# Storing block 0's x, B, C weights, block 0's z through ScalarE, two query loads, and a dealt gate norm in a hybrid attention and state-space layer

## The chip, the cores and the metric

The kernel runs on one core of a Trainium2 chip. The metric is the device time of one launch in microseconds (us). A core has five engines that matter here: TensorE (PE in the profile, matmuls from SBUF into PSUM), VectorE (DVE), ScalarE (ACT), GpSimd (POOL) and SyncE (SP), whose queue issues the DMA transfers. Each engine runs its own instructions in program order and waits on semaphores for the others.

## The reference, cut to what matters

One layer: 2048 frames of a new stream and 32 frames of a running one, 1024 channels. Half of the mixer is stick-breaking attention (8 heads of 64), half is a Mamba-2 scan (SSD, 8 heads of 64, state 64), both from one input projection; then a gated convolutional MLP.

```python
def mixer(h, k_past, v_past, ssm_h0, conv_prev, p):
    proj = h @ p['w_in']                       # q, k, v, z, xbc, dt_raw in this order
    ...
    attn = stick_breaking(q, q_pos, k_all, v_all, k_pos).reshape(b, l, D_ATT)
    xbc_c, conv_new = causal_dwconv(xbc, conv_prev, p['ssm_conv_w'], p['ssm_conv_b'])
    xbc_c = jax.nn.silu(xbc_c)                 # x (512), B (128), C (128)
    ...
    y, h_fin = ssd_scan(xh, dt, a, bm, cm, ssm_h0)
    y = y + p['d_skip'][:, None] * xh
    y = rmsnorm(y * jax.nn.silu(z), p['g_ssm_out'])
    out = jnp.concatenate([rmsnorm(attn, p['g_attn_out']), y], axis=-1) @ p['w_out']

def layer(x, ...):
    x = x + rmsnorm(mixer(rmsnorm(x, p['g_mix_pre']), ...), p['g_mix_post'])
    return x + rmsnorm(conv_ffn(rmsnorm(x, p['g_ffn_pre']), ...), p['g_ffn_post'])
```

The rows of a normalisation share one factor r = rsqrt(mean of squares + eps), so a projection can be taken of x * gain and multiplied by r afterwards. Block 0 does this.

## The kernel before, in words

**Numbers as pairs.** Every matmul with a weight is three matmuls of float32r parts: high times high, high times low, low times high (`dense`, rows of L173). A weight becomes such a pair by `divide` (L148): ScalarE casts the raw block to its high part (L153), GpSimd subtracts to get the low part (L154), and if a key is given, SyncE stores the pair in DRAM as `wS_<key>` (L157). Later `weight` finds the key and `recall`s the pair by one DMA (L145). In the input phase a weight block is 128 columns by all 8 blocks of 128 channels: 512 KB raw, 1 MB as a pair. There are two raw buffers and three pair buffers.

**Blocks.** `phase_in` goes over four blocks of the sequence (512, 512, 512, and 544 with the running stream's 32 frames). In each it projects x, B, C (six column blocks in the order 4, 5, 0, 1, 2, 3; 4 and 5 are B and C, the tile `bc`; 0 to 3 are x, the tile `xc`). Each column block is 24 matmuls into a PSUM bank `o` (two of these), a ScalarE copy out of it (L397), in block 0 a multiplication by r (L401), four convolution steps on VectorE (L404, L408) and a silu (ScalarE's sigmoid L388, VectorE's product L389), one column block late. Then come v and dt (L432), the scan in chunks of 128 frames (its first product is L520, of C with B; acB is its decay matrix), k and q (stored to DRAM), and the gate. `prep(s + 1)` loads the next block's x, and normalises it (L322); `split` makes its pairs (ScalarE L331, VectorE L332).

**Gate.** `gate` (L631) projects z in four column blocks and multiplies xc by silu(z): sigmoid L653, products L654 and L656. For block 0, L647 first multiplies by r, out of PSUM. For blocks 1 and 2 ScalarE copies z to SBUF (`zc`). `gate_norm` (L661) takes squares, one factor, and per column block a product (L677), a cast (L681) and a subtraction (L683), stored as `yS`. Block 3's gate is not run there: it is handed to the attention phase as a filler.

**Attention.** `heads(s, steps)` walks slots, one per 128 query rows and key block: products z (L890), sigmoids on ScalarE, a running product on VectorE (L741), transposes (L909), two copies (L913 on ScalarE, L914 on VectorE) and the products with v (L931). `steps` filler steps are dealt evenly over the slots: heads(0) has 32 slots and deals the 32 steps of block 3's gate, six matmuls each. Every third slot also advances `sample`, the running stream's attention, whose first work is to zero `qp`, load the query into it head by head (L764) and load keys (L786, tile `sk`). After heads(0) the last gate norm runs to its end, in PSUM bank `u`; then `stream(0)`, the output projection and MLP of block 0, is the filler of heads(1), and so on. The last stream runs alone.

**Order.** The code above is program order; a list scheduler with its own cost estimates then sets each engine's order. `behind(a, b)` adds an order between two instructions without a semaphore of its own.

Of the kernel before, what the change touches and what calls it, by code (L numbers as in the profile page):

```python
# [8 lines left out]
F32 = mybir.dt.float32  # L9
# [3 lines left out]
ALU = mybir.AluOpType  # L13
# [18 lines left out]
P = 128  # L32
D = 1024
KC = D // P
SEQ = 2048
DEC = 32
TOK = SEQ + DEC
NH = 8
DH = 64
# [6 lines left out]
NSB = len(SBS)  # L46
# [23 lines left out]
class Kernel:  # L70
# [77 lines left out]
    def divide(self, pool, raw, m, key=None, tag=None):  # L148

        nc = self.nc  # L150
        w = self.held(pool, tag)
        hi, lo = w[:, 0, :m, :], w[:, 1, :m, :]
        nc.scalar.copy(hi, raw[:, :m, :])  # L153
        nc.gpsimd.tensor_tensor(lo, raw[:, :m, :], hi.bitcast(F32), op=ALU.subtract)  # L154
        if key is not None:
            d = self.dp.tile([P, 2, m, P], F32, name="wS_" + "_".join(map(str, key)))
            nc.sync.dma_start(d[:], w[:, :, :m, :].bitcast(F32))  # L157
            self.kept[key] = d[:]
            if m > UNIT:
                for i in range(0, m, UNIT):  # L160
                    self.kept[(*key[:-1], "part", i)] = d[:, :, i : i + UNIT, :]
        return [(w[:, 0, i, :], w[:, 1, i, :]) for i in range(m)]
# [102 lines left out]
def phase_in(kn, ctx):  # L265
    nc, tc, a, o = kn.nc, kn.tc, kn.a, kn.o
    pool = lambda name, bufs, **kw: ctx.enter_context(tc.tile_pool(name=name, bufs=bufs, reuse_waits="tile", **kw))
# [6 lines left out]
    wp = kn.wp  # L274
# [88 lines left out]
        else:  # L363
            nc.scalar.copy(dst, ps)

    wfirst = kn.weight(wp, a["wbx"][4])
    for s, (t0, nt) in enumerate(SBS):
        last = s == NSB - 1
        if s == 0:
            xs, r0 = first()  # L370
# [17 lines left out]
            kn.behind(nc.scalar.activation(t[:, :W], y, AF.Sigmoid), copy)  # L388
            nc.vector.tensor_tensor(y, y, t[:, :W], op=ALU.mult)  # L389

        for c in (4, 5, 0, 1, 2, 3):
            w = wfirst if s == 0 and c == 4 else kn.weight(wp, a["wbx"][c], key=("bx", c) if s or c in (1, 2, 3) else None)
            for c0, c1 in tiles_of(nt):
                ps = psd.tile([P, 512], F32, name="o")
                kn.dense(ps, w, xs, c0, c1)
                e = min(c1, 512)
                copy = nc.scalar.copy(raw[:, c, 3 + c0 : 3 + e], ps[:, : e - c0])  # L397
                if c1 > 512:
                    copy = nc.scalar.copy(raw[:, c, 518:550], ps[:, e - c0 : c1 - c0])
            if s == 0:  # L400
                nc.vector.tensor_tensor(raw[:, c, 3 : 3 + nt], raw[:, c, 3 : 3 + nt], r0[:, :nt], op=ALU.mult)  # L401
            y = xc[:, c, :W] if c < 4 else bc[:, c - 4, :W]
            wc = C_SW + c * 4
            nc.vector.tensor_scalar(  # L404
                y, raw[:, c, 0:W], kn.col(wc), kn.col(C_SB + c), op0=ALU.mult, op1=ALU.add
            )
            for i in range(1, 4):
                nc.vector.scalar_tensor_tensor(  # L408
                    y, raw[:, c, i : i + W], kn.col(wc + i), y, op0=ALU.mult, op1=ALU.add
                )  # L410
            if owed is not None:
                silu(owed, copy)
            owed = y
        if last:
            nc.sync.dma_start(o["sconv"][0], raw[:, :, 512:515])
            nc.sync.dma_start(o["sconv"][1], raw[:, :, 547:550])
        else:
            nc.vector.tensor_copy(hist[:], raw[:, :, 512:515])
# [58 lines left out]
        ps = psm.tile([P, 512], F32, name="st")  # L477
# [140 lines left out]
        if last:  # L618
            return lambda tm, pool: (
                gate(kn, s, xs, xc, None, tm),  # L620
                gate_norm(kn, s, xc, tm, lambda sq, *r: kn.rstd_narrow(pool, *kn.bank, [sq], *r)),
            )
        bufs = {"khi": 2, "klo": 2, "t": 2, "sq": 1, "zc": 2}
        tm = lambda nm: (so if nm in ("khi", "klo") else tmp).tile([P, 550 if nm == "t" else 544], F32, name=nm, bufs=bufs[nm])
# [6 lines left out]
def gate(kn, s, xs, xc, r0, tm):  # L631
# [3 lines left out]
    for c in range(4):  # L635
        w = kn.weight(kn.wp, kn.a["wz"][c], key=("z", c) if s < NSB - 1 else ("z", c, "part"))
        for c0, c1 in tiles:
# [4 lines left out]
                if len(tiles) == 1 or k % 2:  # L642
                    yield
            t = tm("t")
            if r0 is not None:
                z = tm("t")
                nc.vector.tensor_tensor(z[:, :n], ps[:, :n], r0[:, c0:c1], op=ALU.mult)  # L647
                ps = z
            elif s < NSB - 1:
                z = tm("zc")  # L650
                nc.scalar.copy(z[:, :n], ps[:, :n])
                ps = z
            nc.scalar.activation(t[:, :n], ps[:, :n], AF.Sigmoid)  # L653
            nc.vector.tensor_tensor(t[:, :n], ps[:, :n], t[:, :n], op=ALU.mult)  # L654
# [3 lines left out]
                nc.gpsimd.tensor_tensor(xc[:, c, 512:544], xc[:, c, 515:547], t[:, e - c0 : n], op=ALU.mult)  # L658


def gate_norm(kn, s, xc, tm, rstd):  # L661

    nc, nt = kn.nc, SBS[s][1]
    sq = tm("sq")
    for c in range(4):
# [5 lines left out]
            nc.gpsimd.tensor_tensor(sq[:, :nt], sq[:, :nt], t[:, :nt], op=ALU.add)  # L671
        yield
    r = rstd(sq, nt, 512)
    for c in range(4):
        yield
        n = xc[:, c, :nt] if s == NSB - 1 else tm("zc")[:, :nt]
# [11 lines left out]
class Attention:  # L688
# [60 lines left out]
    def sample(self, ctx, pu):  # L749
# [9 lines left out]
            )  # L759
        qp = kp.tile([P, 4, DH], F32, name="qp", bufs=1)  # L760
        nc.vector.memset(qp[:], 0.0)
        for h in range(NH):
            r = slice(64 * (h % 2), 64 * (h % 2) + 64)
            nc.sync.dma_start(qp[r, h // 2, 32 * (h % 2) : 32 * (h % 2) + 32], kn.qF[r, h // 2, :])  # L764
        own = []
        for g in range(2):
            own.append([kp.tile([P, w], F32, name=f"{nm}{g}", bufs=1) for nm, w in (("sgam", 513), ("sbeta", 512), ("sprow", 513))])
# [731 lines left out]
def build(nc, tc, a, o):  # L1499
    kn = Kernel(nc, tc, a, o)  # L1500
    with ExitStack() as ctx:
# [24 lines left out]
        att = Attention(kn, heads)  # L1526
        kn.bank = pu, "u"
        late = ssd.enter_context(tc.tile_pool(name="ssd_tmp", bufs=2, reuse_waits="tile", side="right"))
        att.filler, normed = rest(lambda nm: late.tile([P, 544], F32, name=nm, bufs=1 if nm == "sq" else 2), late)
        with ExitStack() as c2:  # L1530
            sample = att.sample(c2, pu)

            out = att.heads(0, KC * 4, lambda i: i % 3 == 2 and next(sample, None))
            for _ in sample:
                pass
        for _ in normed:
            pass
        ssd.close()
        tail = Tail(kn, att, ctx, pu)
        for s in range(NSB):  # L1540
# [106 lines left out]
```

## Time and profile before

| what | us |
|---|---|
| median of three runs | 2916.16 |
| lowest and highest of them | 2910.60, 2920.89 |
| the profiled execution, its own time | 2923.02 |
| its span, first to last instruction | 2921.2 |
| VectorE, ScalarE, GpSimd busy | 1636.6, 1221.8, 1151.0 |

The profile comes from one execution. Times in its rows count from the span's start. Block 0 of the input phase lasts to about 181, blocks 1, 2 and 3 to about 320, 480 and 606; heads(0) follows to about 735. "PEclk" is the share of full clock that TensorE was granted in a stretch. "`<-`" in brackets names what an engine waited for before the row. PE's matmuls overlap, so rows of them may overlap too. SPq rows are DMA issues, not transfers.

### The profile page before, as it was taken

How to read it: one execution, taken by the hardware profiler on the slowest of the kernel's cores; microseconds unless marked ns; L12 is line 12 of the kernel's file. 1: busy time of each engine (PE TensorE's matmuls, PEld its weight loads, DVE VectorE, ACT ScalarE, POOL GpSimd, SP SyncE). 2: the span in 40 equal slices, each digit the busy share in tenths (PEclk: the TensorE clock that was granted, in tenths of full speed). 3: DMA queues.
4: the chain of work that ended last, by engine and by line, in shares of the span. 5: the costliest groups of instructions: out<-in, count | busy, mean ns of one | idle time of the engine just before them, and what ended most of it. 6: DMA issues, size and time to landing. Idle time of an engine off the chain costs nothing.

```text
span 2921.2 us, 46172 instructions
## 1 busy us (share of the span) xinstructions
PE 2806.3 (96%) x16771; PEld 2427.1 (83%) x16771; DVE 1636.6 (56%) x2628; ACT 1221.8 (42%) x2575; POOL 1151.0 (39%) x1076
## 2 busy tenths in 40 slices
PE   7989999979899999999899999989999999999998
PEld 6768889967878888897788888978888889899997
DVE  7584747448664545457454556776666653623333
ACT  4343434247665545455333334654444443321211
POOL 4634242225766656555322223453322323411113
PEclk9999999999989999999999999999999999999999
DMA  7878776868677777785655556666555555755556
GB/s 270 266 267 245 238 241 205 235 191 289 241 249 256 267 275 257 254 284 186 211 176 175 183 181 227 205 197 200 171 164 172 169 167 189 238 180 180 170 177 205
DMA packets 336708, 632.08 MB, mean 216 GB/s; under 512 B 73594, under 2 KB 193026, under 8 KB 328162
## 3 DMA queue, kind: packets, MB, share of 16 engines
q1 hardware_dynamic: 336482, 629.13, 66.4%
q8 instruction: 134, 2.20, 0.3%
q14 instruction: 92, 0.75, 0.1%
HBM read 472.44 MB, written 156.57 MB: 215 GB/s over the span
## 4 chain that ended last, share of the span: by engine, by line
PE 78%; DMA 9%; DVE 7%; SPq 2%; ACT 2%; issue 2%; POOL 1%; DVEq 0%; ACTq 0%; POOLq 0%
PE o L173 39%; PE u L173 12%; PE t L173 11%; PE z L890 4%; PE pa L931 4%; PE pt L909 3%; PE o L432 3%; DMA acB<-acD 2%; DMA w<-wS_out 1%; DVE prow L741 1%; DMA xr<-hS 1%; DMA wraw<-wbx 1%; DVE xlo L1079 1%; DMA o_kT<-kf 1%; PE u L215 1%
## 5 line engine op out<-in xcount | busy, mean ns | idle before, releaser
L173 PE MATMUL o<-xhi,w 128*128 128x512 f32 (+2 forms) x3968 | 1047.2, 345 | 28.8 <-ACT xhi L346 7.7
L173 PEld LDWEIGHTS o<-xhi,w 128*128 128x128 f32 x3968 | 698.1, 191 | 121.6 <-issue 10.8
L173 PE MATMUL o<-xlo,w 128*128 128x512 f32 (+2 forms) x1984 | 683.0, 344 | 3.0 <-DVE xlo L1079 1.6
L746 POOL TENSOR_TENSOR beta<-beta,prow 128x512 f32<-128x512 f32 (+3 forms) x256 | 255.4, 998 | 448.2 <-DVE prow L741 365.8
L173 PEld LDWEIGHTS o<-xlo,w 128*128 128x128 f32 x1984 | 379.4, 191 | 46.7 <-DVE xlo L1079 2.4
L173 PE MATMUL o<-ah,w 128*128 128x512 f32 x992 | 345.0, 404 | 8.2 <-DVE f L1375 6.8
L173 PE MATMUL u<-xhi,w 128*128 128x512 f32 x1056 | 348.7, 397 | 0.0
L154 POOL TENSOR_TENSOR w<-wraw,w 128x512 fp32r<-128x512 f32 (+3 forms) x189 | 253.8, 1346 | 163.9 <-ACT w L153 143.0
L1327 POOL TENSOR_TENSOR y<-y,gb 128x512 f32<-128x512 f32 (+1 forms) x88 | 115.9, 1317 | 508.4 <-ACT gb L1326 508.2
L914 DVE TENSOR_TENSOR wt<-pt,wt 128x512 fp32r<-128x512 f32 (+2 forms) x320 | 191.2, 601 | 170.3 <-ACT wt L913 168.2
L741 DVE TENSOR_TENSOR_SCAN prow<-gam,prow,z 128x513 f32<-128x513 f32 x192 | 245.1, 1277 | 60.9 <-ACT beta L739 57.1
L913 ACT CAST wt<-pt 128x512 fp32r<-128x512 f32 (+2 forms) x320 | 167.1, 526 | 220.6 <-PE pt L909 219.3
L173 PEld LDWEIGHTS u<-xhi,w 128*128 128x128 f32 x1056 | 198.8, 188 | 46.7
L173 PEld LDWEIGHTS o<-ah,w 128*128 128x128 f32 x992 | 187.7, 189 | 50.6 <-DVE f L1375 8.3
L738 ACT ACTIVATE gam<-z 128x512 f32<-128x512 f32 (+2 forms) x320 | 172.7, 540 | 100.2 <-PE z L890 57.0
L173 PE MATMUL u<-xlo,w 128*128 128x512 f32 x528 | 209.3, 396 | 0.0
L173 PE MATMUL o<-al,w 128*128 128x512 f32 x496 | 197.2, 398 | 0.0
L173 PE MATMUL t<-xhi,w 128*128 128x272 f32 x960 | 189.2, 293 | 2.8 <-DMA w<-wS_up 1.8
L153 ACT CAST w<-wraw 128x512 fp32r<-128x512 f32 (+3 forms) x189 | 117.5, 622 | 169.2 <-PE o L173 103.5
L931 PE MATMUL pa<-wt,v 128*64 128x256 f32 (+3 forms) x1152 | 174.1, 282 | 11.6 <-DVE wt L914 10.6
L909 PE MATMUL pt<-ident,beta 128*128 128x128 f32 x1088 | 180.9, 278 | 2.3 <-DVE wt L914 1.9
L1319 DVE SCALAR_TENSOR_TENSOR y<-gb,cv,y 128x512 f32<-128x512 f32 (+1 forms) x176 | 142.2, 808 | 68.4 <-ACT y L1317 65.9
(285 smaller groups left out, 4899.5 us busy)
## 6 DMA issues: line engine op xcount, KB each, us to landing
w<-wS_up SPq DMA_DIRECT2D x264, 512.0 KB, 3.5
w<-wS_dn SPq DMA_DIRECT2D x144, 384.0 KB, 3.5
wS_up<-w SPq DMA_DIRECT2D x88, 512.0 KB, 3.5
w<-wS_out SPq DMA_DIRECT2D x78, 512.0 KB, 6.1
wraw<-wup SPq DMA_DIRECT2D x88, 256.0 KB, 4.1
k<-kS SPq DMA_DIRECT2D x80, 256.0 KB, 3.8
v<-vS SPq DMA_DIRECT2D x80, 256.0 KB, 3.7
wS_dn<-w SPq DMA_DIRECT2D x48, 384.0 KB, 3.1
```

What stands on the lines that cost most here:

```text
L153: nc.scalar.copy(hi, raw[:, :m, :])
L154: nc.gpsimd.tensor_tensor(lo, raw[:, :m, :], hi.bitcast(F32), op=ALU.subtract)
L173: mm = nc.tensor.matmul(ps[:, : c1 - c0], l, r, start=first and i == 0 and k == 0, stop=last and i == 2 and k == len(w) - 1, **({"skip_gro ...
L738: nc.scalar.activation(g[:, c0:512], z, AF.Sigmoid, scale=-0.125)
L741: nc.vector.tensor_tensor_scan(back(pr), back(g), z[:, 0:1].to_broadcast([P, n + 1]), self.kn.ones[:, 0:1] if prev is None else prev, op0= ...
L746: eng.tensor_tensor(b[:, :n], b[:, :n], pr[:, c0 + 1 : 513], op=ALU.mult)
L890: mm = nc.tensor.matmul(z[:, :n], q[:, P * b : P * b + P], k[:, :n], start=e == 0, stop=e == 1 and kc < s)
L909: mm = nc.tensor.transpose(t[:, P * j : P * j + P], w[:, P * j : P * j + P], kn.ident[:])
L913: nc.scalar.copy(hi, t)
L914: nc.vector.tensor_tensor(lo, t, hi.bitcast(F32), op=ALU.subtract)
L931: nc.tensor.matmul(av[:m, 2 * P * p + c0 : 2 * P * p + 2 * P], v[:, j, :m], wt[:, rest, j, c0:], start=kc == s and p + j + rest == 0, stop ...
L1319: nc.vector.scalar_tensor_tensor(y[:, :W], gb[:, i : i + W], kn.col(wc + i), y[:, :W], op0=ALU.mult, op1=ALU.add)
```

## The change

Four edits:

1. In block 0 all six x, B, C weights get a key, so the pairs of 4, 5 and 0 are stored too, and block 1 recalls all six. Also in block 0, the next column block's weight (`ahead`) is loaded, cast and subtracted in program order before the current matmuls, and the exit copy is put behind its cast.
2. Block 0's z is copied out of PSUM by ScalarE, as in blocks 1 and 2, and multiplied by r in SBUF.
3. `qp` is loaded by two DMAs (all even heads, all odd heads) instead of eight.
4. The last gate norm becomes part of heads(0)'s filler: 4 steps of squares, 4 empty steps (`rests`) behind its factor, 4 steps of products, so 44 in all, and its factor uses the PSUM bank `o`.

```diff
--- before.py
+++ after.py
@@ -150,7 +150,7 @@
         nc = self.nc
         w = self.held(pool, tag)
         hi, lo = w[:, 0, :m, :], w[:, 1, :m, :]
-        nc.scalar.copy(hi, raw[:, :m, :])
+        self.cast = nc.scalar.copy(hi, raw[:, :m, :])
         nc.gpsimd.tensor_tensor(lo, raw[:, :m, :], hi.bitcast(F32), op=ALU.subtract)
         if key is not None:
             d = self.dp.tile([P, 2, m, P], F32, name="wS_" + "_".join(map(str, key)))
@@ -363,7 +363,7 @@
         else:
             nc.scalar.copy(dst, ps)
 
-    wfirst = kn.weight(wp, a["wbx"][4])
+    wfirst = kn.weight(wp, a["wbx"][4], key=("bx", 4))
     for s, (t0, nt) in enumerate(SBS):
         last = s == NSB - 1
         if s == 0:
@@ -388,13 +388,21 @@
             kn.behind(nc.scalar.activation(t[:, :W], y, AF.Sigmoid), copy)
             nc.vector.tensor_tensor(y, y, t[:, :W], op=ALU.mult)
 
-        for c in (4, 5, 0, 1, 2, 3):
-            w = wfirst if s == 0 and c == 4 else kn.weight(wp, a["wbx"][c], key=("bx", c) if s or c in (1, 2, 3) else None)
+        order = (4, 5, 0, 1, 2, 3)
+        w = wfirst if s == 0 else None
+        for c, then in zip(order, (*order[1:], None)):
+            if w is None:
+                w = kn.weight(wp, a["wbx"][c], key=("bx", c))
+            ahead = None
+            if s == 0 and then is not None:
+                ahead = kn.weight(wp, a["wbx"][then], key=("bx", then))
             for c0, c1 in tiles_of(nt):
                 ps = psd.tile([P, 512], F32, name="o")
                 kn.dense(ps, w, xs, c0, c1)
                 e = min(c1, 512)
                 copy = nc.scalar.copy(raw[:, c, 3 + c0 : 3 + e], ps[:, : e - c0])
+                if ahead is not None:
+                    kn.behind(copy, kn.cast)
                 if c1 > 512:
                     copy = nc.scalar.copy(raw[:, c, 518:550], ps[:, e - c0 : c1 - c0])
             if s == 0:
@@ -411,6 +419,7 @@
             if owed is not None:
                 silu(owed, copy)
             owed = y
+            w = ahead
         if last:
             nc.sync.dma_start(o["sconv"][0], raw[:, :, 512:515])
             nc.sync.dma_start(o["sconv"][1], raw[:, :, 547:550])
@@ -618,7 +627,7 @@
         if last:
             return lambda tm, pool: (
                 gate(kn, s, xs, xc, None, tm),
-                gate_norm(kn, s, xc, tm, lambda sq, *r: kn.rstd_narrow(pool, *kn.bank, [sq], *r)),
+                gate_norm(kn, s, xc, tm, lambda sq, *r: kn.rstd_narrow(pool, kn.po, "o", [sq], *r), 4),
             )
         bufs = {"khi": 2, "klo": 2, "t": 2, "sq": 1, "zc": 2}
         tm = lambda nm: (so if nm in ("khi", "klo") else tmp).tile([P, 550 if nm == "t" else 544], F32, name=nm, bufs=bufs[nm])
@@ -642,13 +651,11 @@
                 if len(tiles) == 1 or k % 2:
                     yield
             t = tm("t")
-            if r0 is not None:
-                z = tm("t")
-                nc.vector.tensor_tensor(z[:, :n], ps[:, :n], r0[:, c0:c1], op=ALU.mult)
-                ps = z
-            elif s < NSB - 1:
+            if s < NSB - 1:
                 z = tm("zc")
                 nc.scalar.copy(z[:, :n], ps[:, :n])
+                if r0 is not None:
+                    nc.vector.tensor_tensor(z[:, :n], z[:, :n], r0[:, c0:c1], op=ALU.mult)
                 ps = z
             nc.scalar.activation(t[:, :n], ps[:, :n], AF.Sigmoid)
             nc.vector.tensor_tensor(t[:, :n], ps[:, :n], t[:, :n], op=ALU.mult)
@@ -658,7 +665,7 @@
                 nc.gpsimd.tensor_tensor(xc[:, c, 512:544], xc[:, c, 515:547], t[:, e - c0 : n], op=ALU.mult)
 
 
-def gate_norm(kn, s, xc, tm, rstd):
+def gate_norm(kn, s, xc, tm, rstd, rests=0):
 
     nc, nt = kn.nc, SBS[s][1]
     sq = tm("sq")
@@ -671,6 +678,8 @@
             nc.gpsimd.tensor_tensor(sq[:, :nt], sq[:, :nt], t[:, :nt], op=ALU.add)
         yield
     r = rstd(sq, nt, 512)
+    for _ in range(rests):
+        yield
     for c in range(4):
         yield
         n = xc[:, c, :nt] if s == NSB - 1 else tm("zc")[:, :nt]
@@ -759,9 +768,9 @@
             )
         qp = kp.tile([P, 4, DH], F32, name="qp", bufs=1)
         nc.vector.memset(qp[:], 0.0)
-        for h in range(NH):
-            r = slice(64 * (h % 2), 64 * (h % 2) + 64)
-            nc.sync.dma_start(qp[r, h // 2, 32 * (h % 2) : 32 * (h % 2) + 32], kn.qF[r, h // 2, :])
+        for e in range(2):
+            r = slice(DH * e, DH * e + DH)
+            nc.sync.dma_start(qp[r, :, DEC * e : DEC * e + DEC], kn.qF[r, :, :])
         own = []
         for g in range(2):
             own.append([kp.tile([P, w], F32, name=f"{nm}{g}", bufs=1) for nm, w in (("sgam", 513), ("sbeta", 512), ("sprow", 513))])
@@ -1526,15 +1535,13 @@
         att = Attention(kn, heads)
         kn.bank = pu, "u"
         late = ssd.enter_context(tc.tile_pool(name="ssd_tmp", bufs=2, reuse_waits="tile", side="right"))
-        att.filler, normed = rest(lambda nm: late.tile([P, 544], F32, name=nm, bufs=1 if nm == "sq" else 2), late)
+        att.filler = chained(*rest(lambda nm: late.tile([P, 544], F32, name=nm, bufs=1 if nm == "sq" else 2), late))
         with ExitStack() as c2:
             sample = att.sample(c2, pu)
 
-            out = att.heads(0, KC * 4, lambda i: i % 3 == 2 and next(sample, None))
+            out = att.heads(0, KC * 4 + 12, lambda i: i % 3 == 2 and next(sample, None))
             for _ in sample:
                 pass
-        for _ in normed:
-            pass
         ssd.close()
         tail = Tail(kn, att, ctx, pu)
         for s in range(NSB):
```

SyncE and ScalarE at the front of block 0. SyncE's rows before, from behind the second raw weight and the first wv part (`wraw<-wbx` is a raw x, B, C weight, `wS_bx` a stored pair, `x<-xT` a quarter of block 1's input, `wk` a weight of k):

```order
L130 DMA wraw<-wbx 128x1024 x2
L294 DMA wvraw<-wv 128x1040
L311 DMA x<-xT 128x2x512 x2
L130 DMA wraw<-wbx 128x1024
L311 DMA x<-xT 128x2x512 x2
L157 DMA wS_bx_0_353<-w 128x2048
L130 DMA wraw<-wbx 128x1024
L294 DMA wvraw<-wv 128x1040
L157 DMA wS_bx_0_394<-w 128x2048
L130 DMA wraw<-wk 128x1024
L157 DMA wS_bx_0_435<-w 128x2048
```

and after, from the same place (each `wS_bx` is the pair of one weight, in the order 4, 5, 0, 1, 2):

```order
L157 DMA wS_bx_0_160<-w 128x2048
L130 DMA wraw<-wbx 128x1024
L157 DMA wS_bx_0_246<-w 128x2048
L130 DMA wraw<-wbx 128x1024
L294 DMA wvraw<-wv 128x1040
L311 DMA x<-xT 128x2x512 x4
L157 DMA wS_bx_0_284<-w 128x2048
L130 DMA wraw<-wbx 128x1024
L157 DMA wS_bx_0_325<-w 128x2048
L130 DMA wraw<-wbx 128x1024
L294 DMA wvraw<-wv 128x1040
L157 DMA wS_bx_0_366<-w 128x2048
```

Three more stores stand in the queue, each ahead of the next raw weight, and block 1's input is now loaded ahead of the raw weight of column block 2 in one piece.

ScalarE there, before, from the cast of weight 2 (L153; L260 copies r, L295 casts a wv part):

```order
L153 CAST w<-wraw 128x1024
L397 COPY raw<-o 128x512
L260 COPY r_229<-st 128x512
L153 CAST w<-wraw 128x1024
L397 COPY raw<-o 128x512
L295 CAST wvhi<-wvraw 128x1040
L153 CAST w<-wraw 128x1024
L397 COPY raw<-o 128x512
L388 ACT_TABLE_LOAD
L388 ACTIVATE t<-bc 128x512 x2
```

and after (from the exit copy, now L403, on):

```order
L403 COPY raw<-o 128x512
L260 COPY r_231<-st 128x512
L153 CAST w<-wraw 128x1024
L403 COPY raw<-o 128x512
L388 ACT_TABLE_LOAD
L388 ACTIVATE t<-bc 128x512
L153 CAST w<-wraw 128x1024
L388 ACTIVATE t<-bc 128x512
L295 CAST wvhi<-wvraw 128x1040
L388 ACTIVATE t<-xc 128x512
L403 COPY raw<-o 128x512
```

The exit copies follow casts of a later weight, and the cast of weight 3 (the second L153 here; before it stood ahead of the table load) now follows the table load and the first sigmoid of bc.

VectorE at the end of block 0's gate. Before, from the last chunk of the scan (L564, L567) on; L322 normalises block 1's input, L332 splits it:

```order
L532 TENSOR_TENSOR acB<-acB,cbm 128x512 x2
L564 SCALAR_TENSOR_TENSOR xc<-xc,cv,eA 128x128 x4
L322 SCALAR_TENSOR_TENSOR x<-x,cv,rstd 128x512 x8
L647 TENSOR_TENSOR t<-o,r_229 128x512
L567 TENSOR_TENSOR xc<-y,xc 128x4x128
L654 TENSOR_TENSOR t<-t 128x512
L656 TENSOR_TENSOR xc<-xc,t 128x512
L647 TENSOR_TENSOR t<-o,r_229 128x512
L654 TENSOR_TENSOR t<-t 128x512
L656 TENSOR_TENSOR xc<-xc,t 128x512
L647 TENSOR_TENSOR t<-o,r_229 128x512
L332 TENSOR_TENSOR xlo_1611<-x,xhi_1603 128x512
```

and after (L658 multiplies z by r, L661 and L663 are the two products):

```order
L573 SCALAR_TENSOR_TENSOR xc<-xc,cv,eA 128x128 x4
L658 TENSOR_TENSOR zc<-zc,r_231 128x512
L661 TENSOR_TENSOR t<-zc,t 128x512
L576 TENSOR_TENSOR xc<-y,xc 128x4x128
L663 TENSOR_TENSOR xc<-xc,t 128x512
L658 TENSOR_TENSOR zc<-zc,r_231 128x512
L661 TENSOR_TENSOR t<-zc,t 128x512
L322 SCALAR_TENSOR_TENSOR x<-x,cv,rstd 128x512 x8
L663 TENSOR_TENSOR xc<-xc,t 128x512
L658 TENSOR_TENSOR zc<-zc,r_231 128x512
L332 TENSOR_TENSOR xlo_1621<-x,xhi_1613 128x512
```

The eight L322 moved from ahead of the first z to behind the second, and no row reads z out of PSUM.

VectorE where the last gate norm's products stand. Before, in heads(1) (L741 is the running product of a slot, L914 half of its copy):

```order
L914 TENSOR_TENSOR wt<-pt,wt 128x4x128
L741 SCALAR_TENSOR_TENSOR prow<-gam_5846,ones,z 128x129
L746 TENSOR_TENSOR beta<-beta,prow 128x128
L914 TENSOR_TENSOR wt<-pt,wt 128x4x128
L741 SCALAR_TENSOR_TENSOR prow<-gam_5844,ones,z 128x257
L914 TENSOR_TENSOR wt<-pt,wt 128x4x128
L741 SCALAR_TENSOR_TENSOR prow<-gam_5845,ones,z 128x385
L677 SCALAR_TENSOR_TENSOR xc<-xc,cv,rstd 128x544 x4
L914 TENSOR_TENSOR wt<-pt,wt 128x4x128
L228 TENSOR_SCALAR rn_v<-u 128x2
L741 SCALAR_TENSOR_TENSOR prow<-gam_5846,ones,z 128x513
```

and after, in heads(0) (L750 is the running product, `sprow` that of the running stream):

```order
L923 TENSOR_TENSOR wt<-pt,wt 128x4x128
L750 SCALAR_TENSOR_TENSOR prow<-gam_5841,ones,z 128x513
L923 TENSOR_TENSOR wt<-pt,wt 128x128
L955 TENSOR_TENSOR att<-pa,att 64x512
L923 TENSOR_TENSOR wt<-pt,wt 128x2x128
L686 SCALAR_TENSOR_TENSOR xc<-xc,cv,rstd 128x544 x4
L750 SCALAR_TENSOR_TENSOR sprow_5992<-sgam_5990,scarry_5995,z 128x513
L750 SCALAR_TENSOR_TENSOR prow<-gam_5839,ones,z 128x129
L750 SCALAR_TENSOR_TENSOR prow<-gam_5840,ones,z 128x257
L923 TENSOR_TENSOR wt<-pt,wt 128x3x128
L750 SCALAR_TENSOR_TENSOR prow<-gam_5841,ones,z 128x385
```

The four products moved ahead by about 11 running products; they still stand in one piece.

## The prediction

> **What bounds the kernel now.** I read the page first: span, busy shares and the chain that ended last.
>
> ```profile
> span 2921.2 us, 46172 instructions
> ...
> PE 2806.3 (96%) x16771; PEld 2427.1 (83%) x16771; DVE 1636.6 (56%) x2628; ACT 1221.8 (42%) x2575; POOL 1151.0 (39%) x1076
> ...
> PE 78%; DMA 9%; DVE 7%; SPq 2%; ACT 2%; issue 2%; POOL 1%; DVEq 0%; ACTq 0%; POOLq 0%
> ```
>
> TensorE (PE) is busy for 96% of the span and holds 78% of the chain. The change removes no matmul, so it can only close holes in TensorE's work: 2921.2 - 2806.3 = 115 us in all. Next I read TensorE's waits over the first 900 us, where every edit lies. The columns are total, times, longest.
>
> ```profile
> PE z L789 <- DMA sk<-kF: 7.0, 1, 7.0
> PE pa L931 <- DVE wt L914: 6.3, 2, 4.8
> PE o L173 <- DVE t L647: 6.0, 1, 6.0
> ...
> PE y L520 <- DVE bc L389: 2.5, 1, 2.5
> PE o L173 <- DMA w<-wS_bx: 2.3, 1, 2.3
> ```
>
> Four of these five belong to the edited places: L789 to the query loads, L931 to the gate norm, L647 to block 0's z, wS_bx to the weights. The sum of the four longest waits is 7.0 + 4.8 + 6.0 + 2.3 = 20 us. Third view: windows over these holes and the stretches behind them (length, TensorE busy, granted clock, DMA share, GB/s).
>
> ```profile
> 55.00:58.00 3.00, 3.00 (x16) 0.51 0.68 259
> 160.80:163.60 2.80, 2.78 (x7) 0.50 0.68 234
> 190.80:193.60 2.80, 0.48 (x3) 1.00 1.01 427
> 193.60:197.00 3.40, 3.40 (x10) 0.63 0.81 335
> 616.30:623.20 6.90, 0.02 (x1) 0.85 0.10 15
> 623.20:628.00 4.80, 4.80 (x21) 0.50 0.87 256
> 735.10:739.80 4.70, 0.00 (x0) 0.72 0.53 205
> 739.80:745.00 5.20, 5.03 (x21) 0.59 0.40 134
> ```
>
> A hole costs twice here: behind each, the matmuls run for 3 to 5 us at about half clock. That is (1 - 0.50) x 2.8 = 1.4 us behind the z hole, 0.37 x 3.4 = 1.3 behind the recall, 0.5 x 4.8 = 2.4 behind the query loads. Even the 2.5 and 2.3 us waits (L520, wS_bx) are followed by 0.51 and 0.63.
>
> **1. Block 0's x, B, C weights.** Three more stores of 1 MB in block 0; in block 1 three weights come back by one load of 1 MB each, in place of a raw load, a cast (L153), a subtraction (L154) and a store. In block 0 each weight's load, cast and subtraction are issued ahead of the matmuls of the column block before it, and that block's exit copy stands behind the cast.
>
> ```profile
> 15.60 6.14 POOL L154 TENSOR_TENSOR w<-wraw,w 128x1024 fp32r<-128x1024 f32 x2 [6.51 <-ACT w L153]
> ...
> 31.21 1.05 ACT L153 CAST w<-wraw 128x1024 fp32r<-128x1024 f32 x1 [2.67 <-DMA wraw<-wbx]
> ...
> 39.54 1.05 ACT L153 CAST w<-wraw 128x1024 fp32r<-128x1024 f32 x1 [6.31 <-DMA wraw<-wbx]
> ...
> 40.67 2.42 POOL L154 TENSOR_TENSOR w<-wraw,w 128x1024 fp32r<-128x1024 f32 x1 [5.94 <-ACT w L153]
> ...
> 46.06 1.28 ACT L388 ACT_TABLE_LOAD   x1
> 48.96 0.63 ACT L388 ACTIVATE t<-bc 128x512 f32<-128x512 f32 x1 [1.62 <-DVE bc L408]
> ...
> 41.10 2.53 DVE L401 TENSOR_TENSOR raw<-raw,r 128x512 f32<-128x512 f32 x1 [0.60 <-ACT raw L397]
> ...
> 32.20:48.40 16.20, 16.20 (x72) 1.00 0.91 346
> ...
> 100.00:150.00 50.00, 48.26 (x291) 36.61 (x289) 36.08 (x81) 15.93 (x23) 25.04 (x16) 1.00 0.98 321
> ```
>
> The first window says that column blocks 1, 2 and 3 (72 matmuls, 5.4 us each) ran from 32.2 to 48.4 without a hole; their weights were ready in time. A loaded queue moves 427 GB/s (window 190.8), so 512 KB take 1.2 us and 1 MB 2.5. In the new SyncE order the store of column block 5 waits for its subtraction (ends at 15.60 + 6.14 = 21.74), and behind it stand a raw weight, one wv part, four x loads, the store of block 0 and then the raw weight 2: 2.5 + 1.2 + 1.2 + 4.9 + 2.5 + 1.2 = 13.5, so weight 2 lands near 36, against 31.2. Cast 1.05 and subtraction 2.4 put its third matmul at 39.6, where TensorE arrives at 37.6: **2 us** of waiting. Weight 3's cast now stands on ScalarE behind the table load and the first sigmoid of bc. I put that sigmoid at 44.5: before it ran at 48.96 after VectorE had lost some 2 us to each of the operations that took 2.5 (L401 above; 0.68 is usual for this size, as in L647 below), and fewer of them now come ahead. Then cast to 46.2, subtraction to 48.7: matmuls that ended at 48.4 end near 54. Since the scan's first products (L520) move in among them, their own 2.5 us wait lies inside this one. Net, the step behind L520 begins some 3 us later, and 1 us more goes in half clock: **+4**, from 0 (loads early, sigmoid early) to +10 (bc no earlier than before, two more holes at half clock). From there on TensorE hardly waits (48.26 of 50 us busy up to 150), so nothing takes this back.
>
> In block 1 the wait for wS_bx goes, with its half clock: -2.3 - 1.3 = **-3.6**. Its three recalls are issued ahead of block 2's x loads, and no cast or subtraction replaces them. They hide behind the end of block 0's gate; without this cover the old 2.3 returns.
>
> **2. Block 0's z.** VectorE (DVE) read z out of PSUM (L647), and stood in eight L322 while TensorE wanted the bank.
>
> ```profile
> 152.62 7.46 DVE L322 SCALAR_TENSOR_TENSOR x<-x,cv,rstd 128x512 f32<-128x512 f32 x8
> 160.00 0.68 DVE L647 TENSOR_TENSOR t<-o,r 128x512 f32<-128x512 f32 x1
> ...
> 160.71 0.63 ACT L653 ACTIVATE t<-t 128x512 f32<-128x512 f32 x1 [4.84 <-DVE t L647]
> ...
> 183.45 0.57 ACT L397 COPY raw<-o 128x512 f32<-128x512 f32 x1
> ...
> 178.94 2.78 DVE L656 TENSOR_TENSOR xc<-xc,t 128x512 f32<-128x512 f32 x1
> ...
> 178.19 2.98 POOL L154 TENSOR_TENSOR w<-wraw,w 128x1024 fp32r<-128x1024 f32 x1 [3.44 <-ACT w L153]
> ```
>
> Now a ScalarE copy frees the bank. ScalarE gains four copies (0.57 us, as L397), where it sat idle for 4.84 us before the first sigmoid; VectorE keeps its count. The hole of 6.0 and its 1.4 at half clock go. What is late next is the normalised input of block 1: the L322 now come after the second z, some 5 us later, and block 1's split (L332, eight of 0.68) behind them. TensorE has the third and fourth z (10.3 us) and finds the first split operands about 1.5 us late: -7.4 + 1.4 = **-6**, from -2 (the split sets the start) to -7.4.
>
> The last two rows carry a rule: an L656 that began inside a GpSimd (POOL) subtraction took 2.78 and ended as that ended. The Trainium skill (SBUF — State Buffer, "SBUF: two separate sides") says that a VectorE operation with two SBUF inputs and a GpSimd operation that reads SBUF exclude each other for a whole instruction. That speaks against this edit, since z leaves PSUM before it is multiplied: by the page each of four multiplies may lose up to 2 us, on VectorE alone. By the rows the next operation, L656, has two such inputs already. I leave the sum as it is.
>
> **3. Two query loads instead of eight.**
>
> ```profile
> 616.05 4.92 SPq L764 DMA_DIRECT2D qp<-qF  x8
> 621.01 1.06 SPq L786 DMA_DIRECT2D sk<-kF  x2
> ...
> 623.18 0.39 PE L789 MATMUL z<-sk,qp 128*64 128x32 f32 x2 [6.97 <-DMA sk<-kF]
> ```
>
> SyncE spends 4.92 / 8 = 0.62 us on each issue, and the loads that TensorE waits for are queued behind all eight. Six fewer: 6 x 0.62 = **-3.7**. qp's zeroing lets the first go no earlier than 616.05. The hole shrinks to 3.2 us; a 2.3 us wait already cost half clock above, so I keep the 2.4 behind it. Bounds: 0 (the larger loads land that much later) and -6.1.
>
> In the Trainium skill (TensorE: Matmul & The Clock Gate, "Why this matters for your kernels") gaps under about 3 us keep the clock. By that page a slightly smaller hole would spare the 2.4 too. The trace disagrees: waits of 2.5 and 2.3 us were followed by 0.51 and 0.63.
>
> **4. The last gate norm dealt.** It ran after the first heads; now 12 more steps go into the 32 slots of that pass (a slot is one L890 pair of products), so the gate is done after slot 25, not 31.
>
> ```profile
> 733.76 5.43 DVE L677 SCALAR_TENSOR_TENSOR xc<-xc,cv,rstd 128x544 f32<-128x544 f32 x4
> ...
> 690.30:708.00 17.70, 17.70 (x145) 1.00 0.97 321
> ...
> 716.60:754.70 38.10, 30.10 (x170) 0.78 0.61 203
> ...
> L890 PE MATMUL z<-k,qa x16: 327/482/796, 716.6 to 754.7; 128*128 128x512 f32 x10, 128*128 128x128 f32 x2, 128*128 128x256 f32 x2, 128*128 128x384 f32 x2
> ```
>
> The six slots to 708.0 have gate matmuls: 17.70 / 6 = 2.95 us each, TensorE full. The next window holds 15 slots without filler: 2.54 us each, or 2.2 without the hole behind L677, with 30.1 x 0.78 / 15 = 1.6 us of work at full clock. In the new order there are 26 filled and 18 bare slots before the first output stream's matmuls, where there were 32 and 19. Those 7 slots save 6 x 2.2 + 2.5 = 15.7 (the gate's own 0.75 per slot remains) and cost 7 x 1.6 = 11.2 beside the stream: -4.5. The four L677 still stand in one block on VectorE, so I leave their hole. I take **-4**, from -9 (hole gone) to +2 (it grows by one or two scans queued behind the block).
>
> The edits also reorder other instructions of blocks 1 to 3 without a pattern; I put that at 0, give or take 4.
>
> **Sum.** +4 - 3.6 - 6 - 3.7 - 4 = -13.3 against 2923.0, the profiled execution's own time (2 us lie around its span). That execution was slower than the three timed runs (2910.6, 2916.2, 2920.9); the middle of all four is 2918.5. I set the sum against it: 2918.5 - 13.3 = **2905 us**.
>
> **Rivals.**
> - *VectorE takes the place of the holes.* Block 0's bc comes no earlier (+7), block 1's split sets its start (-2), the L677 block eats the dealing (0). With recall and queries (-7.3): -2.3, **2916**. For it: the three places wait on VectorE by the waits above. Against: it is busy 56%.
> - *The norm is not really dealt.* Its four L677 stay together, and the stream begins no sooner in time. Part 4 is 0: -9.3, **2909**. Against: the stream's matmuls do stand 7 slots earlier.
> - *Holes close wholly.* Front +2, z -7.4, recall -3.6, queries -6.1, norm -8: -23, **2895**. For it: every half-clock stretch above lies behind a hole. The rule of the Trainium skill quoted above (TensorE: Matmul & The Clock Gate, same section) speaks for the queries' share of it.
> - *Slower: holes move and the clock halves behind them.* A hole of some 2.3 us is enough. Two new ones in the front give +10; z's hole shrinks to 3 us and keeps its clock loss (-3); recall and queries stay at -7.3. At half clock throughout, the 15 bare slots' 1.6 x 15 = 24 us of work take 48 in place of 30.1, of which 8.0 fit into their idle time: +9.9, or +12 for 18 slots. Sum +11.7, **2930**. It decides once the front's two waits pass 2.3 us each and the bare slots' clock falls below the 0.78 of now.
>
> **How the numbers follow.** Forecast 0.42; the norm not dealt 0.13; VectorE 0.20; holes closed 0.13; slower 0.12. A measurement of this kernel can tell about 0.3% (8.7 us) from no change, so faster means below 2907.4 and slower above 2924.9. With some 6 us around each case, faster holds 0.26 + 0.05 + 0.02 + 0.13 = 0.46; slower 0.09 + 0.03 = 0.12; the rest, 0.42, is the same. From 2893 to 2924 I leave out most of the slower case and some of the fastest: under 2 in 10.
>
> **What would show it.** Right: no TensorE wait for z's reader in block 0 and none for wS_bx in block 1; clock 1.00 in the fourth z; the wait for sk near 3 us with 0.5 behind it; the stream's first L173 sooner after the last gate matmul's slot. In the front, TensorE waits of about 2 and 3 to 4 us for weights 2 and 3. Wrong: a front wait above 5 us, block 1's first matmuls waiting for xlo by more than 3 us, or a sk wait still near 7.

## The result, and the profile after

The changed kernel took 2896.35 us, the median of nine runs (2890.86 to 2909.14); the kernel before 2918.42 (2910.60 to 2925.64). The ratio is 0.994, with a 95% interval from 0.9922 to 0.9958: 17.5 us less, between 12 and 23 (the two medians alone lie 22 us apart). A second set (e9 below) gave 0.9922 (0.9907 to 0.9938). The profiled execution of the changed kernel was the slowest of its nine (2909.14), so its trace is used for places, and that of e9 beside it for sums.

TensorE's waits in the first 900 us, in the view that the prediction began with:

```profile
PE z L899 <- DVE prow L750: 8.5, 12, 2.5
PE o L173 <- ACT xhi L346: 7.9, 1, 7.9
PE o L173 <- POOL w L154: 4.3, 2, 3.2
PE pa L940 <- DVE att L955: 4.2, 1, 4.2
PE pa L940 <- DVE wt L923: 3.9, 4, 1.7
...
PE z L798 <- DMA sk<-kF: 2.7, 1, 2.7
PE o L173 <- DVE xlo L332: 2.5, 1, 2.5
```

The four waits that the prediction summed have all changed. (The wait for xhi stands at the kernel's start and was there before, with 7.7 us; the prediction's "four longest" leaves it out, and no edit touches it.) The reader of z waits for nothing in block 0, wS_bx is gone, the wait for sk fell from 7.0 to 2.7, the longest wait for wt from 4.8 to 1.7. New are the waits for a weight's subtraction (3.2) and for xlo (2.5), both named in the prediction, and more of the many short ones for prow in heads(0): 8.5 us in twelve, before 4.5 in six.

To see where time came from I laid each trace over that of the kernel before: for a moment in the kernel before I took the moment at which the other had sent the same number of columns through TensorE. The difference is its lead in us, worked out from the start times of all 16771 matmuls.

| lead at (us of the kernel before) | 60 | 140 | 200 | 590 | 850 | 1320 | 1460 | 2200 | 2500 | 2910 |
|---|---|---|---|---|---|---|---|---|---|---|
| changed, first profile | -3.4 | -1.6 | 8.7 | 7.6 | 7.4 | 8.0 | 12.7 | 15.8 | 16.4 | 14.8 |
| changed, e9 | -3.0 | -0.9 | 7.1 | 5.8 | 14.0 | 14.7 | 20.0 | 22.3 | 30.9 | 25.5 |

The two executions of one program differ by up to 14.5 us (at 2500), so a lead read from one trace is good to some 5 us, except in stretches where traces agree. These two agree on three: late by 3 in the front, early by 7 to 9 at 200, and 5 us of lead more from 1320 to 1460. From 590 to 850 the second wins 8 us and the first nothing; the wait for att in the view above (4.2 us, at 753) is in the first of the two alone. Where two orders differ, equal columns are not the same work, so leads inside heads(0) swing more. The stretch from 1320 to 1460 is the end of heads(1), where the change edits nothing.

### The profile page after: what moved, and what is told of

It is laid out like the page before. It is cut to its first block, busy times and chain, and to the rows that moved or that the text cites. A ratio compares the mean times of both kernels' runs of the same rounds, so it can differ in the third digit from the quotient of the medians.

```text
span 2907.1 us, 46192 instructions
## 1 busy us (share of the span) xinstructions
PE 2803.7 (96%) x16771; PEld 2421.8 (83%) x16771; DVE 1644.0 (57%) x2628; ACT 1223.9 (42%) x2576; POOL 1136.7 (39%) x1073
## 4 chain that ended last, share of the span: by engine, by line
PE 80%; DMA 7%; DVE 7%; ACT 3%; issue 2%; SPq 1%; POOL 1%; DVEq 0%; ACTq 0%; POOLq 0%
PE o L173 40%; PE u L173 12%; PE t L173 11%; PE z L899 4%; PE pa L940 4%; PE pt L918 3%; PE o L441 3%; DMA acB<-acD 1%; DVE prow L750 1%; DMA o_kT<-kf 1%; DMA eA<-acD 1%; DVE xlo L1088 1%; DMA xr<-hS 1%; DVE f L1416 1%; PE u L215 1%
## 5 line engine op out<-in xcount | busy, mean ns | idle before, releaser
L1336 POOL TENSOR_TENSOR y<-y,gb 128x512 f32<-128x512 f32 (+1 forms) x88 | 116.2, 1320 | 507.9 <-ACT gb L1335 507.8
L154 POOL TENSOR_TENSOR w<-wraw,w 128x512 fp32r<-128x512 f32 (+3 forms) x186 | 244.4, 1318 | 136.1 <-ACT w L153 116.4
L750 DVE TENSOR_TENSOR_SCAN prow<-gam,prow,z 128x513 f32<-128x513 f32 x192 | 245.3, 1278 | 79.1 <-ACT beta L748 76.3
L153 ACT CAST w<-wraw 128x512 fp32r<-128x512 f32 (+3 forms) x186 | 114.4, 615 | 154.0 <-PE o L173 92.7
```

What stands on the lines that cost most here:

```text
L750: nc.vector.tensor_tensor_scan(back(pr), back(g), z[:, 0:1].to_broadcast([P, n + 1]), self.kn.ones[:, 0:1] if prev is None else prev, op0= ...
L1336: nc.gpsimd.tensor_tensor(y[:, :W], y[:, :W], t, op=ALU.mult)
```

## The experiments

**Each part alone (e1 to e4).** Each is the kernel before with one of the four parts of the diff shown above, unchanged. One line of each:

```diff
+                ahead = kn.weight(wp, a["wbx"][then], key=("bx", then))        # e1, with the rest of part 1
+                    nc.vector.tensor_tensor(z[:, :n], z[:, :n], r0[:, c0:c1], op=ALU.mult)   # e2, part 2
+            nc.sync.dma_start(qp[r, :, DEC * e : DEC * e + DEC], kn.qF[r, :, :])     # e3, part 3
+        att.filler = chained(*rest(...))                                       # e4, part 4
```

> Only part 1, the x, B, C weights of block 0 stored, the next weight ahead and the exits behind its cast. Theory A (the prediction's sum): the front of block 0 is some 4 us late, block 1's wait for wS_bx goes, -3.6, so the time stays within 2 us of the kernel before. Theory B (from the trace of the changed kernel, where TensorE's work was 8 us late at 50 us and only 2 us late at 140): the front costs 2 us or less by the end of block 0, so -2 to -4 us. Rival C (the order of blocks 1 to 3 decides): several us either way that appear behind 200 us.

> Only part 2, block 0's z copied by ScalarE. Theory A: -6 us, of which 6.0 is the wait for L647 and 1.4 the half clock behind it, less 1.4 for a split that comes late. Theory B (the gain at block 0's gate in the changed kernel was 7 us at 170 us and 4.5 at 180 to 190): -4 to -5 us, with a new wait of TensorE for xlo (L332) of some 2.5 us. Rival C: within 2 us of before, because block 1's split sets its start.

> Only part 3, two query loads. Theory A: -3.7 us, the hole shrinks to 3.2 us and the half clock behind it stays. Theory B (in the changed kernel 9 us ahead at 575 became 16 at 640): -6 to -7 us, the clock stays up. Rival C: nothing, since the filler gate takes the hole in another way. Nothing else of the program moves, so no difference should arise before 600 us.

> Only part 4, the last gate norm dealt into heads(0). Theory A (the prediction's): -4 us by 800 us. Theory B (in the changed kernel the lead fell from 16 us at 690 to 7.4 at 850): +4 to +9 us at 850, the slots without filler cost more than the earlier stream brings; at 1400, where heads(1) ends, some 4 us come back. Rival C: 0 at 850, and the loss there in the changed kernel belongs to the other three edits' shift in time.

| kernel | median us | ratio to before (95%) | us less |
|---|---|---|---|
| e1, weights | 2903.93 | 0.9958 (0.9942 to 0.9974) | 12 |
| e2, z | 2918.42 | 1.0007 (0.9995 to 1.0019) | -2 |
| e3, queries | 2897.03 | 0.9936 (0.9918 to 0.9953) | 19 |
| e4, norm | 2903.25 | 0.9966 (0.9949 to 0.9982) | 10 |

(The median of the kernel before in this set was 2914.3; "us less" is 1 - ratio times that.) Three parts alone bring 10 to 19 us each, 41 in sum, and all four together bring 17, or 23 in the second set. Little of what was put down came: e2 fell to its rival C, e1 and e3 brought more than either of their theories A and B, and e4 gained at 850 where its theory B had a loss. Query loads that shortened one hole by 4 us cannot have brought 19. The leads say where the rest is:

| lead at | 60 | 140 | 200 | 590 | 850 | 1320 | 1460 |
|---|---|---|---|---|---|---|---|
| e1, weights | -3.4 | -1.5 | 9.2 | 7.8 | 8.4 | 9.1 | 13.9 |
| e2, z | 0.1 | -0.4 | -2.1 | -6.4 | -8.7 | -8.8 | -8.5 |
| e3, queries | 0.1 | 0.3 | 1.3 | -1.5 | 6.4 | 8.5 | 19.6 |
| e4, norm | 0.4 | 0.6 | 2.0 | 3.0 | 8.2 | 9.7 | 16.5 |

From 1320 to 1460 the three win 4.8, 11.1 and 6.8 us; e2 wins 0.3. I compared the order of TensorE's matmuls, one by one. e2 differs from the kernel before in the z blocks alone. The other three, whatever they edit, differ from it all through heads(0) and heads(1): the scheduler answered each with another order. (So what was written for e3, that nothing else moves, was wrong.) New theory (O): most of the three gains is that order, at the end of heads(1). The prediction had put reordering at 0, give or take 4.

**More loads, and none of the four edits (e5, e6).** e5 doubles the cost that e3 halves; e6 changes only the slots in which the running stream advances. In both, the order of heads(0) and heads(1) changes too.

```diff
 # e5: qp in sixteen loads
         for h in range(NH):
             r = slice(64 * (h % 2), 64 * (h % 2) + 64)
-            nc.sync.dma_start(qp[r, h // 2, 32 * (h % 2) : 32 * (h % 2) + 32], kn.qF[r, h // 2, :])
+            for u in range(2):
+              nc.sync.dma_start(qp[r, h // 2, 32 * (h % 2) + 16 * u : 32 * (h % 2) + 16 * u + 16], kn.qF[r, h // 2, 16 * u : 16 * u + 16])
 # e6: pace alone
-            out = att.heads(0, KC * 4, lambda i: i % 3 == 2 and next(sample, None))
+            out = att.heads(0, KC * 4, lambda i: i % 3 == 1 and next(sample, None))
```

> The kernel before, but the query is loaded by sixteen DMAs instead of eight. Theory Q (the gain of two loads, -17 us, is the queue's time): 8 more issues of 0.62 us put +5 us on the hole, so some +5 us. Theory O (most of the gain of e1, e3 and e4 comes from the list scheduler, which answers each of them with another order of heads(0) to heads(2), and the old order is a bad one): here the order of that stretch also changes, so +5 us at 640, but -5 to -12 us in sum, with the lead coming between 850 and 2500.

> The kernel before, but the running stream's attention advances in slots 1, 4, 7 instead of 2, 5, 8; no instruction is added, removed or made cheaper. From shortly behind heads(0) on, TensorE's order becomes that of the kernel with two query loads. Theory O: -7 to -13 us, again between 850 and 2500. Theory E (the four edits' own local effects make the gains): within 3 us of before.

e5: 2908.15 us, ratio 0.9969 (0.9958 to 0.9979), 9 us less than before although it does more. e6: 2905.26, 0.9952 (0.9934 to 0.9970), 14 us less with no instruction added or removed. Both leads come at the same place: 10.8 and 10.7 us from 1320 to 1460. Theory O holds, with e6 a little above what it allowed (7 to 13); theories Q and E fall.

e5 also measures the price of an issue. Its longest wait of TensorE, from the same view:

```profile
PE z L790 <- DMA sk<-kF: 12.2, 1, 12.2
```

With two loads (e3) the same wait is 2.9, with eight 7.0, with sixteen 12.2: (12.2 - 2.9) / 14 = 0.66 us for each load in front, as the prediction had taken (0.62).

**What is in that stretch.** TensorE's waits from 1310 to 1460, in the kernel before, in e6 and in e9:

```profile
PE z L890 <- DVE rn_v L232: 5.2, 1, 5.2
PE o L173 <- DVE f L1375: 4.7, 3, 3.5
PE pa L931 <- DVE wt L914: 2.2, 2, 2.0
```

```profile
PE u L250 <- POOL rn_v L238: 3.7, 1, 3.7
PE z L890 <- DVE prow L741: 1.9, 2, 1.1
PE o L173 <- DVE f L1375: 1.7, 2, 1.0
```

```profile
PE pa L940 <- ACT wt L922: 4.1, 1, 4.1
PE o L173 <- DVE f L1384: 4.1, 3, 3.3
```

VectorE's rows of the kernel before show what stood in the way:

```profile
1390.82 0.43 DVE L1411 TENSOR_TENSOR f<-f,xr 128x256 f32<-128x256 f32 x1 [4.21 <-DMA xr<-hS]
...
1394.58 1.52 DVE L1411 TENSOR_TENSOR f<-f,xr 128x256 f32<-128x256 f32 x1 [2.73 <-DMA xr<-hS]
...
1396.63 1.27 DVE L741 TENSOR_TENSOR_SCAN prow<-gam,prow,z 128x513 f32<-128x513 f32 x1
1397.82 0.13 DVE L232 SCALAR_TENSOR_TENSOR rn_v<-u,rcol 128x2 f32<-128x2 f32 x1
```

Here stream(0) ends: VectorE adds the residual (L1411) and waits for each piece of it by DMA. Behind two such waits stand heads(1)'s running product and L232, and TensorE's next scores (z, L890) are behind them in turn. They cost more than the idle time, since the clock falls behind the holes:

```profile
1380.00:1400.00 20.00, 14.70 (x69) 0.90 0.56 176
1400.00:1420.00 20.00, 18.05 (x78) 0.84 0.52 159
```

Those are windows of the kernel before. At the same times of e6, by then at other work, TensorE is busier by 2.2 and 1.3 us and the clock at 0.91 and 1.00:

```profile
1380.00:1400.00 20.00, 16.85 (x77) 0.91 0.76 234
1400.00:1420.00 20.00, 19.36 (x94) 1.00 0.77 242
```

Over the same columns, from 1320 to 1460 before and from 1318 to 1447 in e6:

```profile
1320.00:1460.00 140.00, 124.57 (x617) 0.95 0.61 195
```

```profile
1318.00:1447.00 129.00, 120.44 (x590) 0.99 0.67 212
```

TensorE is idle for 15.4 us before and 8.6 in e6, and the work itself takes 4.1 us less at the higher clock: 11 us in all.

In the new orders VectorE still waits for the residual (13 to 14 us in sum, 15 before). What stands behind those waits differs, though not wholly: in e6 one of them, 3.1 us long, still has L232 behind it, and the 3.7 us that TensorE waits for rn_v are at that place. TensorE's order in this stretch falls into groups, word for word the same within each: before and e2 (lead won from 1320 to 1460: 0 and 0.3); e1, e4, e7, e10 and the changed kernel (4.7 to 7.0); e3, e6, e8, e11 (10.7 to 11.8); and e5 by itself (10.8). That the gain is the order is shown by e5 and e6. That it goes by way of the residual waits is read off the rows; no run took those waits away.

**Leaving out one part at a time (e7, e8, then e9 to e12).** The sets e1 to e4, e5 to e8 and e9 to e12 ran on three chips, each beside the kernel before, so sets are compared by their ratios. Each is the changed kernel with one or two parts as before:

```diff
 # e7: part 3 taken back
-        for e in range(2):
-            r = slice(DH * e, DH * e + DH)
-            nc.sync.dma_start(qp[r, :, DEC * e : DEC * e + DEC], kn.qF[r, :, :])
+        for h in range(NH):
+            r = slice(64 * (h % 2), 64 * (h % 2) + 64)
+            nc.sync.dma_start(qp[r, h // 2, 32 * (h % 2) : 32 * (h % 2) + 32], kn.qF[r, h // 2, :])
 # e8 and e12: part 4 taken back
-            out = att.heads(0, KC * 4 + 12, lambda i: i % 3 == 2 and next(sample, None))
+            out = att.heads(0, KC * 4, lambda i: i % 3 == 2 and next(sample, None))
...
+        for _ in normed:
+            pass
 # e10: part 2 taken back; e11: parts 2 and 4
+            if r0 is not None:
+                z = tm("t")
+                nc.vector.tensor_tensor(z[:, :n], ps[:, :n], r0[:, c0:c1], op=ALU.mult)
```

> The changed kernel with the eight query loads of before. Theory Q: 15 us or more slower than the changed kernel, so -3 to -5 us against before. Theory O: it keeps the new order, so only the hole of 3.7 us and at most 2.4 us of half clock return: -12 to -16 us against before.

> The changed kernel with the last gate norm run behind heads(0) as before. Prediction's step 4 (dealing brings 4 us): 4 us slower than the changed kernel, -14 to -18 us against before. Rival D (in the changed kernel the lead fell by 8 us in the bare slots, so dealing costs there): 5 to 8 us faster than the changed kernel, -25 to -28 us. Theory O alone: like the changed kernel within 3 us.

> The changed kernel once more, as the yardstick for the three beside it: -15 to -21 us against before. Nothing in it tells theories apart by itself.

> The changed kernel with block 0's z multiplied out of PSUM as before. Outside the four z blocks every engine's order is that of the changed kernel, so the difference is the z edit's own. Prediction's step 2 (-6 for the z edit): 6 us slower than the changed kernel. Theory S (the weights edit alone has moved L322 behind the second z, and what is left of the hole goes over into the wait for xlo): the same within 2 us, and no wait for L656 above 2 us in its trace.

> Parts 1 and 3 alone. Its order is that of e8 outside the four z blocks. Theory S: as e8, about -22 us against before, so the fastest two kernels of all have no dealt norm. Prediction's step 2: 6 us slower than e8, so -16.

> e8 once more beside the changed kernel, to settle the dealt norm. Rival D (the norm's dealing, with the order of heads(1) that comes with it, costs): 4 to 8 us faster than the changed kernel, of which in the trace the step between 1340 and 1500 is larger by 2 us or less and the rest lies between 640 and 1340. Prediction's step 4: 4 us slower than the changed kernel.

| kernel | median us | ratio to before (95%) | lead won 590 to 850 | 1320 to 1460 |
|---|---|---|---|---|
| e7, without the query loads | 2902.45 | 0.9953 (0.9939 to 0.9967) | 3.9 | 4.9 |
| e8, without the norm | 2895.10 | 0.9923 (0.9909 to 0.9937) | 1.0 | 11.0 |
| e9, changed kernel again | 2894.83 | 0.9922 (0.9907 to 0.9938) | 8.2 | 5.3 |
| e10, without z | 2894.68 | 0.9918 (0.9902 to 0.9935) | 9.2 | 7.0 |
| e11, weights and queries only | 2891.69 | 0.9914 (0.9898 to 0.9930) | 3.6 | 11.8 |
| e12, without the norm again | 2892.55 | 0.9917 (0.9901 to 0.9933) | 3.1 | 11.2 |

*Queries:* without them 0.9953 against 0.994 in the first set: 3.8 us, and 0.9922 in the second set would make it 9; the intervals allow both. Theory O's figure for e7 (12 to 16 us less) holds with 14, theory Q's (3 to 5) does not.

*z:* e10 has the changed kernel's order outside the z blocks, e11 that of e12. Both pairs agree within 0.0004, 1 us. The z edit brings nothing that shows in this kernel, and both pairs speak against the 6 us. The trace of e10 shows why: with L647's form kept, TensorE does not wait for it at all between 140 and 205; its one wait there is

```profile
PE y L569 <- DVE acB L541: 2.0, 1, 2.0
```

*Norm:* with e8 and e12 against the changed kernel's two sets, leaving it out is faster by 5 and 1.5 us, neither clear of noise. That is rival D's direction, but its 4 to 8 us did not come in e12, and the 4 us of the prediction's step came in neither. The leads point to two effects that cancel: dealing wins some 5 us from 590 to 850 (8.2 and 9.2 with it, 3.6 and 3.1 without, in the set of e9 to e12), and its order of heads(1) wins 5 to 7 where the other wins 11 to 12. The second is in every trace. The first rests on this set: the first profile of the changed kernel wins nothing there, and e3, without dealing, wins 7.9.

The best median is that of e11, 2891.69, with parts 1 and 3 alone. Its interval overlaps the changed kernel's: with half the edits it is not shown to be slower or faster.

## Why the prediction came out as it did

The time, 2896, lies inside the range (2893 to 2924), 9 us below the 2905 of the sum, and the gain of 17 us was larger than the forecast of 13. That the sum came so near is partly luck: a term put at 0 brought some 5 us, the z edit brought nothing and the norm nothing that shows, while part 1 alone brought what recall and z were to bring together. The size that failed most is the sentence put beside the four parts.

- **"The edits also reorder other instructions ... I put that at 0, give or take 4."** This failed, and "of blocks 1 to 3" named the wrong place: it is the end of heads(1). e6, with none of the four edits, measures 14 us (9 to 19) for an order, with 10.7 at that place. In the changed kernel the order wins 4.7 to 5.3 there, at the edge of the "give or take 4". The comparison of orders had shown the differences; what I did not do was to look up, in the stretches where the order differs, which waits the old order has. Here they stand in the view of waits: 5.2, 4.7 and 2.2 us.
- **Front, +4.** The starting points came out close, the waits did not, and the bill was smaller. The rows of ScalarE after the change:

```profile
38.04 1.04 ACT L153 CAST w<-wraw 128x1024 fp32r<-128x1024 f32 x1 [5.12 <-DMA wraw<-wbx]
...
44.91 0.63 ACT L388 ACTIVATE t<-bc 128x512 f32<-128x512 f32 x1
45.45 1.03 ACT L153 CAST w<-wraw 128x1024 fp32r<-128x1024 f32 x1
```

  Weight 2 landed at 38.0 (forecast 36), the sigmoid began at 44.9 (44.5), and TensorE waited no longer for bc. Its two waits look like the forecast ones (2 us for weight 2, 3 to 4 for weight 3), but both were for weight 2, first for its cast and then for its subtraction:

```profile
39.14 0.51 PE L173 MATMUL o<-xhi,w 128*128 128x512 f32 x1 [1.48 <-ACT w L153]
...
43.04 1.22 PE L173 MATMUL o<-xhi,w 128*128 128x512 f32 x2 [3.17 <-POOL w L154]
```

```profile
39.16 3.83 POOL L154 TENSOR_TENSOR w<-wraw,w 128x1024 fp32r<-128x1024 f32 x1 [9.97 <-ACT w L153]
```

  The subtraction took 3.8 us where the sum had 2.4. Weight 3 cost no wait: its subtraction ended at 49.2, and TensorE, at a clock of 0.64 from 45 to 50, was busy with weight 2 until 51. It was 3 us late at 60, as forecast, but 1 us or so late at 140 in all six kernels with part 1 that were laid over. So "nothing takes this back" was wrong; some 2 us were taken back.
- **Recall, -3.6, and z, -6: the two together came, by one part.** From 140 to 200 the changed kernel wins 8 to 10 us (forecast 9.6 for the two), and e1, without the z edit, wins 10.7. The term of z failed: alone (e2) it wins nothing. There the copy freed the bank, as the prediction said, but the eight L322 still stood ahead of the first z, and the hole came back in three places. TensorE's waits of e2 from 140 to 205:

```profile
PE o L173 <- DMA w<-wS_bx: 4.7, 1, 4.7
PE o L173 <- DVE xlo L332: 3.2, 3, 2.4
...
PE o L173 <- ACT zc L647: 1.5, 1, 1.5
```

  3.2 + 1.5 and 2.4 more on wS_bx make 7.1, against a hole of 6.0 and its half clock. What the prediction put down to the copy, the L322 behind the second z, comes with part 1: e1 has them there too. Why the scheduler then places them there was not looked into. The first rival, VectorE, came nearest at this place.
- **Queries, -3.7.** Right in size: 0.66 us for each load (e3, e5), and 3.8 us by e7 against the first set. The half clock behind the hole stayed, as taken:

```profile
608.80:611.50 2.70, 0.03 (x1) 1.00 0.27 44
611.50:614.00 2.50, 2.46 (x11) 0.56 0.80 256
614.00:617.00 3.00, 3.00 (x14) 0.50 0.88 281
```

  A hole of 2.7 us, and the clock at 0.50 to 0.56 behind it. The rule of the Trainium skill on gaps under about 3 us (TensorE: Matmul & The Clock Gate, "Why this matters for your kernels") does not hold here. Nor does every such hole cost the clock, as the prediction had it: in the same trace the wait of 2.5 us for xlo, up to 169.1, was followed by 1.00:

```profile
165.00:170.00 5.00, 2.55 (x12) 1.00 0.47 167
170.00:175.00 5.00, 5.00 (x23) 1.00 0.11 44
```

- **Norm, -4.** Its local part has support: with the norm dealt the stream's long run of matmuls begins at 729.0 and 729.3 (e9, e10), without it at 737.0 and 735.6 (e11, e12), and some 5 us of that are left at 850. The hole for wt, which the prediction left in, went from 4.8 to 1.7; the waits for prow grew instead. What it had at 0 is the order that came with the dealing, which won some 5 us less in heads(1) than the other. The net is 0 to +5, so the 0 that the rivals "the norm is not really dealt" and "VectorE" gave this part was nearer than -4, though by another way: the stream does begin sooner.
- **The rivals.** "Holes close wholly" gave 2895, nearest to the median, by another way: the hole of the queries did not close, and no sum of closed holes is behind the number. "Holes move, and the clock halves" had a trace of truth in the front (clock 0.64 from 45 to 50), far below its price.
- The lock between VectorE and GpSimd (Trainium skill, SBUF — State Buffer, "SBUF: two separate sides") was seen again in e2: a multiplication of z from SBUF took 2.52 us in place of 0.68. It did not fall to VectorE alone: the split's first L332 stood behind it, and TensorE waited 0.6 us for that. The 2.4 us wait for xlo came behind an L654 of 2.9 us, likewise begun inside a subtraction. Both are in the 3.2 above.

## What to carry to other kernels

Where a scheduler sets the order, an edit's time has two parts: what it does at its place, and the order that the rest then gets. Compare orders first; where they differ, read the old waits there, and measure the order by itself with a change that does no work, before crediting an edit. Edits tested one by one can each seem to bring the whole of one shared gain: three of them brought 41 us in sum, and all four together 17 to 23.

A copy that frees a buffer moves a hole unless the work that stood ahead of the reader also moves: ask what the next reader waits for, and whether that is late by the same engine.

## What was not expected of the hardware

Two executions of one program came apart by 14.5 us at one moment of the span (first profile and e9, at 2500) though the medians of its two sets, 2896.35 and 2894.83, agree within 0.1%. In e2, whose order behind the z blocks is that of the kernel before, the lead went from -11.0 at 2200 to -2.5 at 2500, so a step there, seen in most traces, is put down to the one profile of the kernel before and not to any edit.
